# A 64-byte against a 192-byte start for x^T, and short matmuls ahead of twelve groups of products

## The chip, the cores and the metric

The kernel runs on one core of a Trainium2 chip. The metric is device time in microseconds (us) of one execution; the time before is the median of three runs, 2145.29 us (2144.81 to 2148.92).

## The reference

Two transformer blocks, one after the other, on 256 tokens of width 2048, all in fp32.

- The first block: RMS norm, a projection `h @ w_in` to 1024 + 2x128 + 3x1024 + 16 columns, a windowed attention with sinks (16 heads on 2 key heads) and a forgetting attention (16 heads), a norm of each, `concat @ w_out`, a residual; then norm, `h @ w_up` (2 x 5632 columns), a causal convolution of width 3 over the tokens, `gelu(gate) * val`, `@ w_down`, a residual.
- The second block: a modulation from `silu(c) @ w_ada`, norm, `h @ w_in_2` for the tokens and the key and value columns of it for 256 context tokens, rotary positions, windowed attention over tokens and context, a pooling path, `concat @ w_out_2`, a residual; then `square(relu(h @ w_mlp_up)) @ w_mlp_down` with 8192 inner columns, a residual and a last norm.

## The kernel before, in words

Every large product of fp32 matrices is made of three passes. Weights and activations are split into a high part (`hi`, rounded to the type fp32r) and a low part (`lo`, what is left), and each product adds hi x hi, hi x lo and lo x hi in a PSUM bank (`products`, L273 to L286 of the profile; all its matmuls have the line L285).

`run` works through a list of groups in order: v, kva, qa, qk0, qk1, wo_a0, wo_a1, wo_b0, wo_b1; up0, up1, up2, then twice-halved w_down groups (dn) that take two up groups each, between up groups: dn0, up3, up4, dn2, up5, up6, dn4, up7, up8, dn6, up9, up10, dn8; ckv, kv, q, u, wo2_p0, wo2_p1, wo2_a0, wo2_a1; mup0, mup1, mdn0, mup2, mdn1, and so on to mup7, mdn6, mdn7. A group's weights arrive in blocks of 1 MB by DMA on SP's queue into `raw` (four buffers); ScalarE rounds each half block into a `hi` tile (L156), VectorE subtracts for the `lo` tile (L168). Each of these has four buffers of 1088 elements of 4 bytes, used in rotation. PACE and `tick` place the side work (attention steps, the modulation's dot products, evacuations) between the halves of a block. The names in the trace are those of the groups without their number: the banks of up0 to up10 are b_up.

There are two kinds of product. In a feature-major one (op "A": kva, qa, qk, up, q, mup, half of ckv and kv) the stationary operand is a 128x128 slice of a weight tile and the moving one is x^T, 256 tokens wide; the trace shows it as `b_up<-a,hi` (moving, stationary). In a token-major one (op "B": v, wo, dn, u, mdn, the other half of ckv and kv) the moving operand is a weight slice of up to 512 columns and the stationary one is 128 tokens of x^T or of another activation; `b_dn<-hi,p`. Each matmul has its own weight load (engine PEld). A group of 1024 feature-major columns has 384 products: 16 slices of the contraction, four banks of two, three passes.

x^T is held as hi and lo tiles from `xt_tile` (L339 to L341), eight slices of 256 tokens to a tile. A tile has 2112 elements of 4 bytes, 8448 bytes, 33 x 256; x^T begins 16 elements, 64 bytes, into it. It is written by `make_ht` (L344): four transposes (L357) a bank, then ScalarE and VectorE. v, kva, qa, qk, up, ckv, kv, q, u and mup read it; wo, dn and mdn read other tiles, which begin at the tile's own start.

Other matmuls of TensorE stand between the products where side work has them: attention's steps in qk (L455, L456 scores on 64 rows; L499 transposes; L511, L514), the decay sums ahead of qa (L735 to L739), the transposes of `make_ht` in up0, mup0, ckv and kv. In up1 to up10 and in mup1 to mup7 there are none.

Of the kernel before, what the change touches and what calls it, by code (L numbers as in the profile page):

```python
# [9 lines left out]
F32R = mybir.dt.float32r  # L10
# [25 lines left out]


WARM = dict(up0=8, mup0=4)


class Group:
# [27 lines left out]
class Kernel:  # L69
# [51 lines left out]
    def run(self, groups):  # L121
        nc = self.nc
        blocks = [(g, b) for g in groups for b in range(g.nb)]
        raws, his, los = {}, [], []
        dma_p = [0]

        def dma_to(i):
            while dma_p[0] <= min(i, len(blocks) - 1):
                g, b = blocks[dma_p[0]]
                self.n += 1  # L130
                t = self.raw_p.tile([128, 2080], F32, tag="raw", name=f"raw{self.n}")
                t3 = t[:, :2 * g.kpc * g.width].rearrange("p (k f) -> p k f", f=g.width)
                if g.middle and b == 0:
                    g.load(t3[:, 0:1], 0)
                    g.between()
                    g.load(t3[:, 1:2], 1)
                else:
                    g.load(t3, b)
                raws[dma_p[0]] = t
                dma_p[0] += 1  # L140

        def part(j):
            i, u = divmod(j, 2)
            g = blocks[i][0]
            w = g.kpc * g.width
            return g.conv or (lambda d, r: [(d, r)]), raws[i][:, u * w:(u + 1) * w], w

        def hi_to(j):
            while len(his) <= min(j, 2 * len(blocks) - 1):
                dma_to(len(his) // 2 + 2)  # L150
                views, raw, w = part(len(his))
                self.n += 1
                hi = self.w_p.tile([128, 1088], F32R, tag="hi", name=f"hi{self.n}")[:, :w]
                with self.behind("hi"):
                    for h, r in views(hi, raw):
                        nc.scalar.copy(h, r)  # L156
                his.append(hi)

        def lo_to(j):
            while len(los) <= min(j, 2 * len(blocks) - 1):  # L160
                n = len(los)
                hi_to(n)
                views, raw, w = part(n)
                self.n += 1
                lo = self.w_p.tile([128, 1088], F32R, tag="lo", name=f"lo{self.n}")[:, :w]
                with self.behind("lo"):
                    for (l, r), (h, _) in zip(views(lo, raw), views(his[n], raw)):
                        self.dve.tensor_tensor(out=l, in0=r, in1=h.bitcast(F32), op=ALU.subtract)  # L168
                los.append(lo)

        banks = None
        for i, (g, b) in enumerate(blocks):
            last = b == g.nb - 1
            if last and g.tail:
                continue
            if not g.middle or b:
                lo_to(2 * i)
            if b == 0 and i and blocks[i - 1][0].tail and not g.prep:
                lo_to(2 * i + 3)
            fresh = b == 0 and i and blocks[i - 1][0].tail and g.prep  # L180
            if not fresh and (b or not g.middle):
                hi_to(2 * i + 3)
            if b == 0:
                self.pace = PACE[g.name] if g.name in PACE else PACE[g.name.rstrip('0123456789')]
                self.ticks = 0
                if not isinstance(self.pace, tuple):
                    self.wait = min(self.wait, self.pace)
                if g.before:
                    g.before()
                if g.side:  # L190
                    self.sides += g.side()
                banks = None
            if fresh:
                self.keep_warm(WARM[g.name], mm)
                g.prep(-2)
                self.held["hi"], self.held["lo"] = [self.ev[0]], [self.ev[1]]
                lo_to(2 * i + 1)
            if g.prep:
                g.prep(b)
            if fresh:  # L200
                hi_to(2 * i + 3)
            if banks is None:
                banks = [self.bank(g.name) for _ in g.banks]
            w2 = [(his[j], los[j]) if j < len(los) else None for j in (2 * i, 2 * i + 1)]

            def unit(bank, prog, u):
                for kk in range(g.kpc):
                    k = (2 * b + u) * g.kpc + kk
                    w = [t[:, kk * g.width:(kk + 1) * g.width] for t in w2[u]]
                    self.products(bank, prog, w, g.xs(k), k == 0, k == g.nk - 1)  # L210

            nb = len(banks)
            if g.tail and b == g.nb - 2:

                w2 = []
                for u in range(4):
                    lo_to(2 * i + u)
                    hi_to(2 * i + 3)
                    w2.append((his[2 * i + u], los[2 * i + u]))
                    for n in range(nb // 2):  # L220
                        unit(banks[n], g.banks[n], u)
                    self.tick(False)
                for n in range(nb):
                    if n >= nb // 2:
                        for u in range(4):
                            unit(banks[n], g.banks[n], u)
                    mm = self.mm
                    g.done(n, banks[n])
                continue
            if g.middle and b == 0:  # L230
                for tt in range(2):
                    if tt:
                        g.middle()
                    for u in range(2):
                        lo_to(2 * i + u)
                        w2[u] = his[2 * i + u], los[2 * i + u]
                        for n in range(nb // 2 * tt, nb // 2 * (tt + 1)):
                            unit(banks[n], g.banks[n], u)
                    hi_to(2 * i + 2 + tt)
                self.tick()  # L240
                lo_to(2 * i + 3)
                continue
            if not last:
                for u in range(2):
                    lo_to(2 * i + u)
                    hi_to(2 * i + u + 3)
                    w2[u] = his[2 * i + u], los[2 * i + u]
                    for bank, prog in zip(banks, g.banks):
                        unit(bank, prog, u)
                    self.tick()  # L250
                    lo_to(2 * i + u + 3)
                continue
            lo_to(2 * i + 1)
            w2 = [(his[j], los[j]) for j in (2 * i, 2 * i + 1)]
            for n, (bank, prog) in enumerate(zip(banks, g.banks)):
                unit(bank, prog, 0)
                unit(bank, prog, 1)
                if n == (nb - 1) // 2 and nb > 1:
                    self.tick()
                    lo_to(2 * i + 3)  # L260
                if g.done:
                    g.done(n, bank)
            self.tick()
            lo_to(2 * i + 3)
            if g.after:
                g.after(banks)
# [6 lines left out]
    def products(self, bank, prog, w, x, first, last):  # L273
        nc = self.nc
        (wh, wl), (xh, xl) = w, x
        for n, op in enumerate(prog):
            passes = ((wh, xh), (wh, xl), (wl, xh))
            for m, (ww, xx) in enumerate(passes):
                if op[0] == "A":
                    _, o, c = op  # L280
                    dst, lhsT, rhs = bank[:, o:o + 256], ww[:, c:c + 128], xx
                else:
                    _, o, w_, tt, c = op
                    dst, lhsT, rhs = bank[:, o:o + w_], xx[:, 128 * tt:128 * tt + 128], ww[:, c:c + w_]
                self.mm = self.pe.matmul(dst, lhsT, rhs, start=first and n == 0 and m == 0,  # L285
                                 stop=last and n == len(prog) - 1 and m == 2, skip_group_check=True)  # L286
# [51 lines left out]

    def xt_tile(self):  # L339

        return self.A8([128, 2112], F32R)[:, 16:16 + 2048].rearrange("p (k t) -> p k t", t=256)  # L341


    def make_ht(self, src, gain, shift=None):  # L344
# [1158 lines left out]
```

## Time and profile before

| what | value |
|---|---|
| median of three runs | 2145.29 us |
| profiled execution, its own time | 2145.99 us |
| span from first to last instruction | 2144.2 us |
| TensorE busy | 2119.4 us |
| VectorE busy | 1576.6 us |
| ScalarE busy | 1077.7 us |
| DMA | 491.39 MB, 229 GB/s in the mean |
| granted clock of TensorE, mean | 0.997 |

An engine's busy time is the union of its instructions' recorded durations. Those of matmuls overlap, as they are pipelined, and their ends are modelled; so the distance between the starts of two products, not their duration, says what a product costs.

### The profile page before, as it was taken

The numbers are of one execution on the slowest core, as the hardware profiler recorded it, in microseconds if no ns is written. First come the engines' busy times: TensorE is split into PE (matmuls) and PEld (weight loads), VectorE is DVE, ScalarE is ACT, GpSimd is POOL, SyncE is SP. The second block draws the span as 40 slices with busy tenths as digits, with TensorE's granted clock in tenths as the row PEclk, the third lists the DMA queues.
The fourth block names the chain that finished last, engine by engine and source line by source line (L and its number), as shares of the span: only waits on it lengthen the run. The fifth ranks groups of instructions, "written<-read, shape, count | busy, mean of one in ns | idle before, by whom it ended". The sixth has DMA issues, their size and how long they took to land.

```text
span 2144.2 us, 34901 instructions
## 1 busy us (share of the span) xinstructions
PE 2119.4 (99%) x14278; PEld 1928.9 (90%) x14278; DVE 1576.6 (74%) x2094; ACT 1077.7 (50%) x1557; POOL 39.3 (2%) x58
## 2 busy tenths in 40 slices
PE   8999999999999999999999999999999999999997
PEld 7998977999998999989989978889898998989986
DVE  6777688788679787797899797765656657555476
ACT  5446565555445543454566466454543434434343
POOL 0001000000000000000000000000000000000000
PEclk9999999999999999999999999999999999999999
DMA  8753576676767788787878754845767677555673
GB/s 308 267 181 136 157 226 227 217 255 225 258 232 248 256 284 305 267 318 278 278 278 283 274 168 158 216 157 181 251 205 273 212 248 246 189 197 179 196 233 101
DMA packets 120960, 491.39 MB, mean 229 GB/s; under 512 B 8736, under 2 KB 12640, under 8 KB 107360
## 3 DMA queue, kind: packets, MB, share of 16 engines
q1 hardware_dynamic: 120800, 489.16, 67.2%
q8 instruction: 112, 1.84, 0.3%
q14 instruction: 48, 0.39, 0.1%
HBM read 484.90 MB, written 2.13 MB: 227 GB/s over the span
## 4 chain that ended last, share of the span: by engine, by line
PE 96%; DVE 2%; ACT 1%; DMA 1%; issue 0%; POOL 0%; POOLq 0%; ACTq 0%; SPq 0%; DVEq 0%
PE b_up L285 23%; PE b_mup L285 17%; PE b_mdn L285 16%; PE b_dn L285 10%; PE b_qk L285 4%; PE b_wo_a L285 4%; PE b_v L285 2%; PE b_u L285 2%; PE b_qa L285 2%; PE b_q L285 2%; PE b_wo_p L285 2%; PE b_wo_b L285 2%; PE b_kv L285 1%; PE b_ckv L285 1%; PE b_aux L1202 1%; PE b_aux L1159 1%
## 5 line engine op out<-in xcount | busy, mean ns | idle before, releaser
L168 DVE TENSOR_TENSOR lo<-raw,hi 128x1024 fp32r<-128x1024 f32 (+2 forms) x716 | 850.4, 1199 | 448.6 <-ACT hi L156 447.1
L156 ACT CAST hi<-raw 128x1024 fp32r<-128x1024 f32 (+2 forms) x716 | 730.4, 1030 | 854.3 <-PE b_up L285 208.5
L285 PE MATMUL b_up<-a,hi 128*128 128x256 f32 x2816 | 499.8, 280 | 0.0
L285 PEld LDWEIGHTS b_up<-a,hi 128*128 128x128 f32 x2816 | 431.2, 188 | 0.5
L285 PE MATMUL b_up<-a,lo 128*128 128x256 f32 x1408 | 393.8, 280 | 0.0
L285 PE MATMUL b_mup<-a,hi 128*128 128x256 f32 x2048 | 363.0, 280 | 1.4 <-ACT a L374 1.4
L285 PE MATMUL b_mdn<-hi,p 128*128 128x512 f32 x1024 | 315.6, 389 | 0.0
L285 PEld LDWEIGHTS b_mup<-a,hi 128*128 128x128 f32 x2048 | 313.2, 187 | 2.1 <-ACT a L374 1.6
L285 PE MATMUL b_mup<-a,lo 128*128 128x256 f32 x1024 | 285.8, 279 | 0.0
L285 PEld LDWEIGHTS b_up<-a,lo 128*128 128x128 f32 x1408 | 265.3, 188 | 0.0
L587 DVE SCALAR_TENSOR_TENSOR raw<-raw,srow 128x2048 f32<-128x2048 f32 x96 | 219.6, 2287 | 25.0 <-DMA raw<-in_w_ada 24.7
L285 PEld LDWEIGHTS b_mdn<-hi,p 128*128 128x128 f32 x1024 | 191.7, 188 | 39.5
L285 PE MATMUL b_dn<-hi,p 128*128 128x512 f32 x704 | 217.2, 390 | 0.0
L285 PE MATMUL b_mdn<-lo,p 128*128 128x512 f32 x512 | 199.2, 389 | 0.0
L285 PEld LDWEIGHTS b_mup<-a,lo 128*128 128x128 f32 x1024 | 192.5, 188 | 0.0
L285 PEld LDWEIGHTS b_dn<-hi,p 128*128 128x128 f32 x704 | 131.6, 188 | 26.9
L285 PE MATMUL b_dn<-lo,p 128*128 128x512 f32 x352 | 137.1, 390 | 0.1
L285 PEld LDWEIGHTS b_mdn<-lo,p 128*128 128x128 f32 x512 | 96.1, 188 | 20.1
L285 PE MATMUL b_qk<-a,hi 128*128 128x256 f32 x512 | 93.4, 283 | 0.0
L285 PE MATMUL b_wo_a<-hi,a 128*128 128x512 f32 x256 | 80.3, 395 | 0.0
L285 PEld LDWEIGHTS b_qk<-a,hi 128*128 128x128 f32 x512 | 77.7, 188 | 2.6 <-issue 2.0
L285 PEld LDWEIGHTS b_dn<-lo,p 128*128 128x128 f32 x352 | 66.1, 188 | 14.4 <-DVE lo L168 0.6
(264 smaller groups left out, 2525.4 us busy)
## 6 DMA issues: line engine op xcount, KB each, us to landing
raw<-in_w_ada SPq DMA_DIRECT2D x96, 1024.0 KB, 5.6
raw<-in_w_up SPq DMA_DIRECT2D x88, 1024.0 KB, 5.0
raw<-in_w_mlp_up SPq DMA_DIRECT2D x64, 1024.0 KB, 5.0
raw<-in_w_mlp_down SPq DMA_DIRECT2D x64, 1024.0 KB, 5.7
raw<-in_w_in SPq DMA_DIRECT2D x50, 1024.0 KB, 5.9
raw<-in_w_down SPq DMA_DIRECT2D x44, 1024.0 KB, 6.2
raw<-in_w_out SPq DMA_DIRECT2D x32, 512.0 KB, 6.7
raw<-in_w_out SPq DMA_DIRECT2D x16, 1024.0 KB, 6.5
```

What stands on the lines that cost most here:

```text
L156: nc.scalar.copy(h, r)
L168: self.dve.tensor_tensor(out=l, in0=r, in1=h.bitcast(F32), op=ALU.subtract)
L285: self.mm = self.pe.matmul(dst, lhsT, rhs, start=first and n == 0 and m == 0, stop=last and n == len(prog) - 1 and m == 2, skip_group_chec ...
L587: self.dve.scalar_tensor_tensor(out=r, in0=r, scalar=1.0, in1=self.srow[0], op0=ALU.mult, op1=ALU.mult, accum_out=self.ada[:, f:f + 1])
L1159: self.pe.matmul(bk.rearrange("p (m c) -> p m c", m=2), qq, k.rearrange("p (m c) -> p m c", m=2)[:, :, o:o + 256], start=n == 0, stop=n == ...
L1202: self.pe.matmul(o[64 * s:64 * s + 64, 128 * qt:128 * qt + 128], v[:, c:c + 64], PT[x][:, 128 * kt:128 * kt + 128], start=kt == 0, stop=kt ...
```

## The change

x^T begins 48 elements, 192 bytes, into its tile instead of 16. And ahead of the first product of twelve groups stand one to four more matmuls (`LEAD`: rows, columns and moving columns of each and how many; 0 moving columns stands for a transpose of the identity). They write the first bank of the group, whose first product then starts it anew.

```diff
+LEAD = dict(qa=(128, 128, 128, 2), up2=(128, 128, 128, 1), up4=(128, 128, 128, 2), up6=(128, 128, 128, 4), up8=(128, 128, 0, 1), q=(128, 128, 64, 2),
+            mup2=(128, 128, 0, 2), mup3=(128, 128, 0, 4), mup4=(64, 128, 128, 1), mup5=(64, 128, 128, 2), mup6=(128, 128, 16, 1), mup7=(128, 128, 16, 4))
...
             if b == 0:
...
                 self.ticks = 0
+                self.lead = LEAD.get(g.name)
...
                     dst, lhsT, rhs = bank[:, o:o + 256], ww[:, c:c + 128], xx
+                    if self.lead:
+                        rows, cols, moving, times = self.lead
+                        self.lead = None
+                        for _ in range(times):
+                            if moving:
+                                self.pe.matmul(bank[0:cols, 0:moving], ww[0:rows, 0:cols], xx[0:rows, 0:moving], start=True, stop=True,
+                                               skip_group_check=True)
+                            else:
+                                self.pe.transpose(bank[:, 0:128], self.ident, self.ident)
...
-        return self.A8([128, 2112], F32R)[:, 16:16 + 2048].rearrange("p (k t) -> p k t", t=256)
+        return self.A8([128, 2112], F32R)[:, 48:48 + 2048].rearrange("p (k t) -> p k t", t=256)
```

## Rows read from the trace of the kernel before

**Rows 1.** The page: engines' busy time and share; chain that ended last, by engine.
```profile
PE 2119.4 (99%) x14278; PEld 1928.9 (90%) x14278; DVE 1576.6 (74%) x2094; ACT 1077.7 (50%) x1557; POOL 39.3 (2%) x58
...
PE 96%; DVE 2%; ACT 1%; DMA 1%; issue 0%; POOL 0%; POOLq 0%; ACTq 0%; SPq 0%; DVEq 0%
```

**Rows 2.** Two stretches: PE, PEld, DVE, ACT, POOL busy (count), PEclk, DMA share, GB/s.
```profile
960.20:1050.60 90.40, 90.40 (x769) 90.40 (x768) 65.72 (x71) 41.16 (x48) 0.00 (x0) 1.00 0.80 284
2000.80:2046.00 45.20, 45.20 (x385) 45.20 (x384) 20.12 (x17) 16.56 (x17) 0.00 (x0) 1.00 0.58 188
```

**Rows 3.** Timeline of TensorE in qk0: start us, duration us, what.
```profile
131.41 0.28 PE L285 MATMUL b_qk<-a,lo 128*128 128x256 f32 x1
...
133.88 0.28 PE L285 MATMUL b_qk<-a,lo 128*128 128x256 f32 x1
...
134.94 0.55 PE L499 MATMUL b_aux<-ident,p 128*128 128x128 f32 x3
...
135.56 0.28 PE L285 MATMUL b_qk<-a,lo 128*128 128x256 f32 x1
...
137.94 0.28 PE L285 MATMUL b_qk<-a,lo 128*128 128x256 f32 x1
```

**Rows 4.** By tile: count, duration ns min/median/max, first and last start us.
```profile
L285 PE MATMUL b_qk<-a,lo x7: 279/279/279, 148.8 to 150.9; 128*128 128x256 f32 x7
...
L285 PE MATMUL b_up<-a,lo x16: 280/280/282, 395.2 to 400.5; 128*128 128x256 f32 x16
...
L285 PE MATMUL b_qa<-a,lo x128: 278/280/280, 78.2 to 123.3; 128*128 128x256 f32 x128
```

**Rows 5.** Timeline of TensorE: decay sums ahead of qa; transposes in up0.
```profile
76.65 0.29 PE L735 MATMUL b_aux<-p,p 128*128 128x16 f32 x2
...
77.01 0.37 PE L737 MATMUL b_aux<-p,p 128*128 128x16 f32 x2
77.24 0.68 PE L738 MATMUL b_aux<-p,p 128*128 128x256 f32 x2
...
394.44 0.28 PE L285 MATMUL b_up<-a,lo 128*128 128x256 f32 x1
394.56 0.60 PE L357 MATMUL b_aux<-ident,a 128*128 128x128 f32 x4
...
395.24 0.28 PE L285 MATMUL b_up<-a,lo 128*128 128x256 f32 x1
```

**Rows 6.** Timeline of TensorE in qk0, score matmuls on 64 rows.
```profile
126.13 0.28 PE L285 MATMUL b_qk<-a,lo 128*128 128x256 f32 x1
126.34 0.48 PE L455 MATMUL b_aux<-p,p 64*128 64x128 f32 x2
126.66 0.59 PE L456 MATMUL b_aux<-p,p 64*128 64x256 f32 x2
...
127.53 0.28 PE L285 MATMUL b_qk<-a,lo 128*128 128x256 f32 x1
```

**Rows 7.** Timeline of TensorE in v and in u.
```profile
50.99 0.49 PE L285 MATMUL b_v<-hi,a 128*128 128x352 f32 x2
...
51.48 0.49 PE L285 MATMUL b_v<-hi,a 128*128 128x352 f32 x2
...
51.97 0.47 PE L285 MATMUL b_v<-hi,a 128*128 128x336 f32 x2
...
1215.65 0.39 PE L285 MATMUL b_u<-lo,a 128*128 128x512 f32 x1
...
1217.75 0.39 PE L285 MATMUL b_u<-lo,a 128*128 128x512 f32 x1
```

**Rows 8.** By tile: the products of mdn1 (columns as in Rows 4).
```profile
L285 PE MATMUL b_mdn<-lo,p x64: 389/389/395, 1602.6 to 1645.4; 128*128 128x512 f32 x64
```

**Rows 9.** Groups by line and shape: count, busy us, mean ns, idle before.
```profile
L285 PE MATMUL b_up<-a,lo 128*128 128x256 f32 x1408 | 393.8, 280 | 0.0
...
L285 PE MATMUL b_mup<-a,lo 128*128 128x256 f32 x1024 | 285.8, 279 | 0.0
```

## The prediction

> **What bounds the kernel now.** I read the page first: its busy line, the granted clock over the 40 slices and the chain that ended last. TensorE is busy for 99% of the span and is 96% of the chain [rows 1]. So the time is a sum of starts on TensorE: whatever shortens or lengthens the step from one product to the next is paid one for one, and nothing else is. Then I read busy time by stretch. A stretch of two feature-major groups, up9 and up10, b_up from 960.2 to 1050.6 us, holds 768 products in 90.4 us, 117.7 ns each, at a granted clock of 1.00 (the 2.4 GHz level); the last b_mup group, 384 products in 45.2 us, gives the same 117.7 ns. VectorE is busy for 65.7 of the 90.4 us, ScalarE for 41.2, the DMA engines for 80% [rows 2]. There are ten such stretches behind w_down and w_mlp_down groups, and all ten run at this pace. The reader is to see that here the engine is neither waiting nor slowed in its clock.
>
> Third, the timeline of TensorE inside b_qk, where attention matmuls cut the same kind of product into short stretches. It shows a second pace. From 131.41 to 133.88 us 21 steps take 2.47 us, 117.6 ns each; from 135.56 to 137.94, behind three transposes, 21 steps take 2.38 us, 113.3 ns each [rows 3]. Same shapes, same tiles, same x^T. So the step has two values, 4.4 ns apart, and the engine keeps the one it entered with: of the 27 stretches of b_qk behind other matmuls, nine run at the fast pace, from their second or third product to their end. What precedes the entry does not settle it alone: also behind three transposes, the stretch from 148.8 us stays slow; b_up behind four transposes is slow (nine such entries in b_up and b_mup, all slow), and so is all of b_qa behind narrow matmuls [rows 4]. In these rows the recorded duration of a product, 279 to 280 ns, marks the slow pace.
>
> **The change, part by part.**
>
> *Leads.* Twelve groups get 26 short matmuls in all (2+1+2+4+1+2 and 2+4+1+2+1+4). All stand on the chain. Each writes the bank that the first real product then clears, reads the weight tile and x^T that this product needs anyway, or the constant identity, and so adds no wait: what the first product waited for, the first lead waits for. It moves no DMA and no work of VectorE or ScalarE. Its price: four transposes of the identity kind put 0.80 us between two products that stand 0.353 us apart otherwise (394.44 to 395.24), so 0.112 us each; of 16-column matmuls the last two take 0.23 us (77.01 to 77.24), again about 0.112 each, and all six 0.59 us, 0.098 each [rows 5]. The column count hardly matters, each brings its own weight load. I take 0.112 for 23 of them: 2.6 us. The three leads on 64 rows are dearer: four 64-row matmuls of attention put 1.40 us between two products otherwise 0.353 apart, 0.262 us each [rows 6]; they stream more columns than the leads do, so this is a high value: 0.8 us. Sum 3.4 us; the ends are 26 x 0.098 = 2.5 us and 26 x 0.262 = 6.8 us.
>
> *What a lead can give back.* A group of 384 products that runs at 113.3 instead of 117.7 ns is 384 x 4.4 = 1.7 us shorter. Of the twelve groups only b_qa is cut by other matmuls of TensorE, once, so what is entered should last to the end of the group; the cover is there, since VectorE, ScalarE and the DMA engines have 20% or more left in rows 2 where 4% are needed. Whether a given lead lands in the fast pace the trace does not show: no short matmul of this operand type stands ahead of such a product. The nearest rows bound it: none of the nine entries behind four transposes, nine of 27 in b_qk [rows 3, 4]. The ends are 0 and 12 groups, 0 and 20.3 us. I take a quarter, three groups, 5.1 us, nearer to b_qk, because most leads are of the same operand type as the products, and no two groups have the same lead.
>
> Here a rule of the notes speaks against the change. The Trainium skill (TensorE: Matmul & The Clock Gate, section Step-by-step: what each phase is for) says that the moving operand and the weight load have independent read ports into SBUF, so that loading the next weights takes no read bandwidth from the running matmul. By it there is one pace, a lead is pure cost, and the sum is +3.4 us. The two paces of rows 3, at one granted clock, do not fit it, though they do not show that the ports are the reason.
>
> *The offset.* x^T moves by 128 bytes; no instruction is added or removed. Its price is in the pace of every product that reads it: as moving operand in the feature-major groups, as stationary one in b_v, b_u and half of b_ckv and b_kv. The best row is b_v: its weights are read in column groups that begin 0 and 1,408 bytes into the tile, and 1,408 is 128 past a multiple of 256. So the two groups already differ by just this shift between moving and stationary operand, and their triples take 0.49 us each (50.99 to 51.48, 51.48 to 51.97) [rows 7]. Hence I take zero. Both are slow: at the pace of b_mdn, 189 steps in 42.8 us or 226.5 ns for 512 columns [rows 8], three products of 352 columns would take 0.467. The bounds: b_u steps 233.3 ns (1215.65 to 1217.75, nine steps) against those 226.5, so 6.8 ns hang on each weight load there [rows 7, 8]; 192 products make 1.3 us, either way. For the feature-major products the ends are the fast pace for all and b_u's loss for all; they are rivals below.
>
> *Sum.* The profiled execution took 2145.99 us, its span 2144.2 and 1.8 around it, 0.7 above the median of the three runs, 2145.29. 2145.99 + 3.4 - 5.1 + 0 = 2144.3; set to the median, **2143.6 us**. With one to four groups landing, 2147.0 to 2141.9. About 0.2%, 4.3 us, is what a measurement of this kernel can tell from no change: below 2141.0 is faster, above 2149.6 slower.
>
> **The rivals.**
>
> *No lead lands: cost alone.* For it: nine entries of nine behind four transposes stayed slow, and all groups behind 512-column products do. Against: nine fast stretches in b_qk. 2145.3 + 3.4 = 2148.7, with the bounds 2147.8 to 2152.1. This is also what the rule of the skill cited above gives.
>
> *Most leads land*, five to twelve: if what counts is just that the first weight load falls beside a short matmul, all are alike. 2145.3 + 3.4 - 8.5 = 2140.2 down to 2145.3 + 3.4 - 20.3 = 2128.4.
>
> *The offset itself sets the fast pace everywhere.* b_up and b_mup have 3 x (1,408 + 1,024) = 7,296 products [rows 9], b_qa 384 [rows 4]: 7,680 x 4.4 = 33.8 us, so 2145.3 - 33.8 + 3.4 = 2114.9. For it: the pace depends on how two streams of reads meet, and the offset moves one of them. Against: b_v's two column groups.
>
> *The other side: the offset makes each product slower.* If relative position counts and its sense matters, a moving x^T 192 past the weights stands as b_u's weights stand now to a stationary x^T that is 64 past them; there each weight load costs 6.8 ns, where the feature-major step now pays 4.4. The difference, 2.4 ns on 7,680 products, is 18.4 us: 2145.3 + 18.4 + 3.4 = 2167.1. The place is every product of b_up and b_mup; it decides early: beyond the 3.4 us of the leads, 0.9 us more, or 0.12 ns a product, carries the time past 2149.6. Against it again b_v, and that b_u's products have 512 columns.
>
> That the leads do nothing because they are dropped can't be: they are plain matmuls in program order.
>
> **How the numbers follow.** Forecast (one to four land) 0.36; none lands 0.16; most land 0.21; offset fast 0.14; offset slow 0.13. Faster: 0.21 + 0.14 + 0.02 for four landing with cheap leads = 0.37. Slower: 0.13 + 0.04 of the cost-alone case at its dear end = 0.17. Same: the rest, 0.46. The range: its low end, 2126, holds "most land" with some room for b_u, and leaves out "offset fast" (0.14). Its high end, 2156, holds cost alone and half of "offset slow", whose 0 to 2.4 ns a product are all open; 0.06 stays out. The likeliest case alone has 2141.9 to 2147.0.
>
> **What would show it.** In the changed kernel's busy time by stretch, a group that landed takes 43.5 us for its 384 products, one that did not 45.2, and the recorded durations turn from 280 to 276. The groups without leads (b_up 1, 3, 5, 7, 9 and 10, b_mup 1) should still take 45.2 each: if they take 43.5, the offset did it; if they take more, the slow rival did. Starts of leads should stand 0.10 to 0.12 us apart. The forecast is wrong if the groups without leads change pace, if none or more than four of the twelve turn, or if a group loses its pace before its end.

## The result, and the profile after

The changed kernel takes 2135.1 us (median of four runs, 2133.43 to 2137.08); the kernel before, beside it, 2145.05 (2144.68 to 2148.92). The ratio is 0.995, its 95% interval 0.9933 to 0.9967: 10 us, 0.5% faster. The profiled execution took 2134.39 us, its span 2132.6, 11.6 below that of before.

The page of the changed kernel, engines' busy time and the chain that ended last, stands against [rows 1].

```profile
PE 2107.4 (99%) x14304; PEld 1917.0 (90%) x14304; DVE 1576.6 (74%) x2094; ACT 1077.9 (51%) x1557; POOL 40.2 (2%) x58
...
PE 95%; DVE 2%; ACT 1%; DMA 1%; issue 0%; POOL 0%; POOLq 0%; ACTq 0%; SPq 0%; DVEq 0%
```

TensorE has 26 instructions more and is busy 12 us less; VectorE and ScalarE have the same work. So the same products were taken at shorter steps. Busy time by stretch says where. Columns as in [rows 2]; in order the stretches are up3, up4, up9 with up10, q, mup1, mup2, mup3 and mup4 of the changed kernel.

```profile
554.90:600.10 45.20, 45.20 (x385) 45.18 (x384) 26.71 (x27) 19.25 (x23) 0.00 (x0) 1.00 0.67 239
600.30:643.90 43.60, 43.60 (x388) 43.60 (x386) 37.42 (x41) 22.02 (x27) 0.00 (x0) 1.00 0.66 228
955.97:1046.40 90.43, 90.43 (x769) 90.41 (x768) 66.12 (x71) 41.05 (x48) 0.00 (x0) 1.00 0.79 284
1166.40:1209.90 43.50, 43.50 (x385) 43.50 (x385) 31.86 (x43) 18.82 (x32) 0.00 (x0) 1.00 0.87 311
1461.20:1504.60 43.40, 43.40 (x385) 43.40 (x384) 24.32 (x25) 20.98 (x25) 0.00 (x0) 1.00 0.59 193
1548.30:1593.60 45.30, 45.30 (x387) 45.30 (x386) 21.97 (x20) 19.28 (x23) 0.00 (x0) 1.00 0.63 214
1637.50:1681.10 43.60, 43.60 (x387) 43.60 (x386) 22.30 (x21) 18.39 (x21) 0.00 (x0) 1.00 0.65 217
1725.00:1768.60 43.60, 43.60 (x385) 43.55 (x385) 22.29 (x21) 18.40 (x21) 0.00 (x0) 1.00 0.64 213
```

The granted clock is 1.00 in all of them, and the same 384 products take 45.2 or 43.5 us. Fast are up4, q, mup3, mup4 and, not shown, mup5, which have leads, and mup1, which has none. Of the other groups with leads mup2 is slow, and so are up2, up6, up8, mup6 and mup7; qa is fast for its first 48 products. The groups without leads up1, up3, up5, up7, up9 and up10 are slow as in [rows 2].

The recorded durations, by tile, mark the pace as in [rows 4]: up3, up4, and the last stretch of qk1.

```profile
L299 PE MATMUL b_up<-a,lo x125: 280/281/282, 555.5 to 599.3; 128*128 128x256 f32 x125
...
L299 PE MATMUL b_up<-a,lo x127: 275/276/277, 600.6 to 643.4; 128*128 128x256 f32 x127
...
L299 PE MATMUL b_qk<-a,lo x39: 275/276/279, 242.8 to 255.7; 128*128 128x256 f32 x39
```

In qk0 and qk1, which have no leads, 16 of the 27 stretches behind other matmuls end at the fast pace, where nine did before.

TensorE's timeline at the entries of up4, mup3 and mup4 (columns as in [rows 3]) shows what stands between the last product of the group before and the first of the new one.

```profile
600.03 0.28 PE L299 MATMUL b_up<-a,lo 128*128 128x256 f32 x1
600.14 0.33 PE L292 MATMUL b_up<-a,hi 128*128 128x128 f32 x2
600.31 0.45 PE L299 MATMUL b_up<-a,hi 128*128 128x256 f32 x2
...
1636.96 0.39 PE L299 MATMUL b_mdn<-lo,p 128*128 128x512 f32 x1
1637.19 0.60 PE L295 MATMUL b_mup<-ident 128*128 128x128 f32 x4
1637.54 0.48 PE L299 MATMUL b_mup<-a,hi 128*128 128x256 f32 x2
...
1724.48 0.39 PE L299 MATMUL b_mdn<-lo,p 128*128 128x512 f32 x1
1724.80 0.32 PE L292 MATMUL b_mup<-a,hi 64*128 64x128 f32 x1
1725.05 0.50 PE L299 MATMUL b_mup<-a,hi 128*128 128x256 f32 x2
```

Two leads of 128 columns push the first product of up4 back by 0.17 us, four transposes that of mup3 by 0.35. A single lead on 64 rows is dearer: it starts 0.32 us behind the last product, where mup3's first transpose starts at 0.23, and the first product comes 0.25 behind it. A further 0.06 to 0.11 us of each lies in the first steps after it: a fast group without leads takes 43.52 us, one behind leads 43.58 to 43.64.

By the distances between the first products of the groups, the 11.6 us are: up4, mup3, mup4 and mup5, 1.6 each, -6.4; q -2.0, mup1 -1.7, mup0 -1.2, v -1.7, qk0 and qk1 -0.9, u -0.5, up0 -0.4, kva and qa -0.4, together -8.8; and about +3.6, of which 0.6 stands in dn80, the first half of the last w_down groups, which differs by that much between runs, and the rest is what the leads cost elsewhere. So the larger part comes from groups that have no lead, and from q. The dn and mdn products keep their 226.7 ns.

### The profile page after: what moved, and what is told of

Its sections match the earlier page's. It is cut to its first block, busy times and chain, and to the rows that moved or that the text cites. A ratio compares the mean times of both kernels' runs of the same rounds, so it can differ in the third digit from the quotient of the medians.

```text
span 2132.6 us, 34950 instructions
## 1 busy us (share of the span) xinstructions
PE 2107.4 (99%) x14304; PEld 1917.0 (90%) x14304; DVE 1576.6 (74%) x2094; ACT 1077.9 (51%) x1557; POOL 40.2 (2%) x58
## 4 chain that ended last, share of the span: by engine, by line
PE 95%; DVE 2%; ACT 1%; DMA 1%; issue 0%; POOL 0%; POOLq 0%; ACTq 0%; SPq 0%; DVEq 0%
PE b_up L299 23%; PE b_mup L299 17%; PE b_mdn L299 16%; PE b_dn L299 9%; PE b_qk L299 4%; PE b_wo_a L299 4%; PE b_u L299 2%; PE b_qa L299 2%; PE b_wo_p L299 2%; PE b_q L299 2%; PE b_v L299 2%; PE b_wo_b L299 2%; PE b_ckv L299 1%; PE b_kv L299 1%; PE b_aux L1216 1%; PE b_aux L1173 1%
## 5 line engine op out<-in xcount | busy, mean ns | idle before, releaser
L299 PE MATMUL b_mup<-a,hi 128*128 128x256 f32 x2048 | 355.6, 279 | 1.3 <-ACT a L388 1.3
L598 DVE SCALAR_TENSOR_TENSOR p<-raw,srow 128x2048 bf16<-128x2048 f32 x32 | 73.2, 2289 | 9.3 <-DMA raw<-in_w_ada 9.1
```

Of the source, the lines that this page charges most:

```text
L598: self.dve.scalar_tensor_tensor(out=junk, in0=r, scalar=1.0, in1=self.srow[1], op0=ALU.mult, op1=ALU.mult, accum_out=self.adac[:, f:f + 1])
```

## The experiments

Each edit is against the changed kernel; in the cuts, lists of group names are written short. "Fast" is 113.3 ns a product (43.5 us for a group), "slow" 117.8 (45.2).

**The offset without leads.**

```diff
-LEAD = dict(qa=(128, 128, 128, 2), ...
+LEAD = {}
```

> x^T at 192 bytes, no lead. Theory (offset and leads act apart): v is 1.7 us shorter as in the changed kernel, kva, qa, qk, u, up0 and mup0 with mup1 together 5.0, all from the offset alone; up2 to up8, q and mup2 to mup7 stay at 117.8 ns; in all 2145.1 - 6.7 = 2138.4 us. Rival (the offset is what makes all fast groups fast): up4, q, mup3, mup4 and mup5 run at 113.3 without their leads as well, five times 1.65 us more, 2130.

Measured: 2137.97 us (2135.25 to 2139.68) against 2145.53; ratio 0.9967, interval 0.9955 to 0.998. Busy time by stretch, up2 and up3:

```profile
464.33:507.85 43.52, 43.52 (x386) 43.52 (x385) 39.33 (x50) 22.31 (x28) 0.00 (x0) 1.00 0.73 247
551.38:596.61 45.23, 45.23 (x385) 45.22 (x384) 27.18 (x29) 19.29 (x23) 0.00 (x0) 1.00 0.68 244
```

By tile, the products of q and of mup1:

```profile
L298 PE MATMUL b_q<-a,lo x128: 276/276/278, 1164.2 to 1207.4; 128*128 128x256 f32 x128
...
L298 PE MATMUL b_mup<-a,lo x127: 276/276/276, 1454.9 to 1497.8; 128*128 128x256 f32 x127
```

Without a lead anywhere, kva, the later part of up0, up1, up2, q and mup1 are fast, and qk is 0.9 us shorter. All groups that come straight behind dn or mdn, and those that follow these (up3 to up10, mup2 to mup7), stay at 45.23. So the offset alone is worth 7.6 us by the medians. The time is the theory's, its places are not: q and up2 were to stay slow. The offset acts where something other than a product of 512 columns stands ahead (transposes, attention, rotary matmuls), and the pace is then handed on: up1 and up2 take it from the end of up0.

What stands ahead can also turn a pace over. Four times in up0 and in mup0, behind their start, four transposes of `make_ht` stand between the products. In mup0 of the changed kernel, by tile, before the first of these entries, behind it, and behind the second:

```profile
L299 PE MATMUL b_mup<-a,lo x24: 275/276/277, 1418.0 to 1425.8; 128*128 128x256 f32 x24
...
L299 PE MATMUL b_mup<-a,lo x15: 280/281/282, 1426.9 to 1431.9; 128*128 128x256 f32 x15
...
L299 PE MATMUL b_mup<-a,lo x15: 276/276/278, 1433.0 to 1437.8; 128*128 128x256 f32 x15
```

So it goes fast, slow, fast, and then slow and fast again. In the nine profiles with x^T at 192 bytes, those of the kernels below among them, there are 72 such entries, and 69 turn the pace over; the other three are each the first of their group. In the three profiles at 64 bytes none of 24 does, and all are slow. How up0 and mup0 end thus hangs on the pace they begin with, which differs between runs. Below, with the 64-row leads behind dn and mdn alone, up0 ends slow, and no lead stands ahead of it there either.

**The leads without the offset.**

```diff
-        return self.A8([128, 2112], F32R)[:, 48:48 + 2048]...
+        return self.A8([128, 2112], F32R)[:, 16:16 + 2048]...
```

> x^T at 64 bytes as before, with the twelve leads. Theory (the kind of lead decides, whatever the offset): up4, q, mup3, mup4 and mup5 run at 113.3 ns, the other seven at 117.8; 5 x 1.65 gained, 3 us paid for the leads, 2145.1 - 5.2 = 2139.9 us. Rival (a lead lands only with the offset at 192): none of the twelve is fast, the leads cost 3 us, 2148.

Measured: 2144.5 us (2141.4 to 2146.22), ratio 0.9996, interval 0.9986 to 1.0005: no difference to be seen. Three groups are fast: up4, mup2 and mup6. Busy time of TensorE by stretch, mup2, mup3 and mup6:

```profile
1557.70:1601.30 43.60, 43.60 (x387) 1.00 0.65 221
1645.20:1690.50 45.30, 45.30 (x387) 1.00 0.61 206
1912.70:1956.30 43.60, 43.60 (x387) 1.00 0.59 191
```

At 192 bytes mup3, mup4 and mup5 land, at 64 bytes mup2 and mup6. The same lead at the same place lands at one offset and not at the other, so the two parts of the change don't act independently. Neither expectation held: the fast groups are others than the theory's, and they are not none. Three groups give back 5.1 us, the leads cost 3.6, and 1.5 us of gain is left to show, which this measurement can't tell from nothing.

**The changed kernel once more**, with nothing edited, to see whether an entry is chance.

> The changed kernel once more, nothing altered. In its first profile up4, q, mup1, mup3, mup4 and mup5 run at 113.3 ns a product, up2, up6, up8, mup2, mup6 and mup7 at 117.8. Theory (the pace is set at a group's entry by what stands there): the same groups at the same paces, 43.5 to 43.7 against 45.2 to 45.4 us each. Rival (chance at each entry): other groups are fast this time; two of these twelve or more change sides.

Measured: 2130.82 us in one run, span 2129.0. Eleven of the twelve groups with leads take the pace that they took before, to 0.01 us. The exception is up6, which is fast this time. The timeline of up5 (no lead of its own) and its tile's rows before and after the wait show how:

```profile
692.02 0.40 PE L299 MATMUL b_up<-a,hi 128*128 128x256 f32 x2
692.95 0.38 PE L299 MATMUL b_up<-a,lo 128*128 128x256 f32 x1 [0.53 <-DVE lo L172]
```

```profile
L299 PE MATMUL b_up<-a,lo x15: 281/281/281, 686.6 to 691.5; 128*128 128x256 f32 x15
...
L299 PE MATMUL b_up<-a,lo x109: 276/276/276, 693.8 to 730.5; 128*128 128x256 f32 x109
```

up5 enters slow, meets a wait of TensorE for VectorE's lo tile after some 50 products, goes on fast for the rest, and hands the pace to up6 through its four leads. So an entry is not drawn by lot; but a wait is an entry too, and waits differ from run to run.

**One kind of lead everywhere:** a single one on 64 rows, ahead of kva, qa, q, up1 to up10 and mup1 to mup7.

```diff
+LEAD = {n: (64, 128, 128, 1) for n in (kva qa up1 ... up10 q mup1 ... mup7)}
```

> x^T at 192 bytes, and one and the same lead, one matmul on 64 rows with 128 columns (that of mup4), ahead of each of 20 groups: kva, qa, up1 to up10, q, mup1 to mup7. Theory (the kind decides): all of up1 to up10, q and mup1 to mup7 run at 113.3 ns, 18 x 1.65 = 29.7 us gained, 20 x 0.3 paid for the leads, and 4 to 5 us of the offset in v, qk, u, up0 and mup0: about 2117 us. Rival (place decides as much as kind): some of these groups stay at 117.8, half of them would give about 2131.

Measured: 2128.82 us (2128.65 to 2129.56), ratio 0.9924, interval 0.991 to 0.9939. Busy time of TensorE by stretch, up3, up4 and mup2:

```profile
554.30:598.20 43.90, 43.90 (x386) 1.00 0.71 252
598.20:643.50 45.30, 45.30 (x385) 1.00 0.66 225
1547.70:1591.30 43.60, 43.60 (x385) 1.00 0.65 215
```

Behind dn and mdn this lead lands ten times out of ten, with the starts of the entries alike to 1 ns. Behind a feature-major group it turns the pace over, seven times of seven: up1, up4, up6, up8, up10 and mup1, each behind a fast end, are slow, and up2, behind the slow up1, is fast. So what stands ahead counts with the lead.

**The same lead behind dn and mdn alone** (up3, up5, up7, up9, mup2 to mup7).

```diff
+LEAD = {n: (64, 128, 128, 1) for n in (up3 up5 up7 up9 mup2 ... mup7)}
```

> x^T at 192 bytes; the lead of one matmul on 64 rows stands only ahead of the ten groups that follow token-major w_down or w_mlp_down products: up3, up5, up7, up9, mup2 to mup7. With it ahead of all groups those ten were fast, and up4, up6, up8, up10 and mup1, each behind a fast feature-major group, were slow. Theory (a group that follows another feature-major one keeps its pace unless other matmuls stand between, and the lead there threw it over): up4, up6, up8, up10 and mup1 run at 113.3 ns without a lead; ten times 1.25 net and four times 1.7 off the kernel with the offset alone, 2138.0 - 19.3 = 2118.7 us. Rival (these five are slow for their place): they stay at 117.8, 2125.5.

Measured: 2124.7 us (2123.61 to 2125.81), ratio 0.9912, interval 0.9896 to 0.9929. Busy time of TensorE by stretch, up3 and up4:

```profile
556.94:600.57 43.63, 43.63 (x386) 1.00 0.68 243
600.57:644.09 43.52, 43.52 (x387) 1.00 0.66 230
```

All ten groups with a lead are fast, and up4, up6, up8 and up10 are fast without any: one feature-major group hands its pace to the next. Each lead costs 0.45 us, 0.34 ahead of the first product and 0.11 in the first steps. up1, up2, mup1 and q, which hang on how up0, mup0 and the rotary matmuls end, are slow in this run (45.23 us, q 45.63). So the time is near the rival's, 2125.5, but of the five groups in question four run as the theory said, and mup1 alone is slow. q has no lead here and is slow, and in the next kernel too.

**Different kinds at those ten places** (one run).

```diff
+LEAD = dict(up3=(128, 128, 128, 1), up5=(128, 128, 128, 2), up7=(128, 128, 128, 4), up9=(128, 128, 64, 2), mup2=(128, 128, 64, 1),
+            mup3=(128, 64, 128, 1), mup4=(128, 128, 0, 1), mup5=(128, 128, 0, 3), mup6=(64, 128, 64, 1), mup7=(128, 128, 16, 2))
```

> x^T at 192 bytes; ahead of the same ten groups ten different leads: up3 one 128x128x128, up5 two, up7 four, up9 two with 64 columns, mup2 one with 64 columns, mup3 one on 128 rows and 64 output columns, mup4 one identity transpose, mup5 three, mup6 one on 64 rows with 64 columns, mup7 two with 16 columns. Theory (what decides is the delay between the last product and the first one's weight load, in steps of some ns): about half of the ten land at 113.3 ns, among them mup6, whose delay is that of the 64-row lead; each of up4, up6, up8, up10 has the pace of the group before it. Rival (only 64-row leads and four transposes land, because they interrupt the overlap of weight loads and products): mup6 alone lands.

Measured: 2126.05 us. Fast: up5 (two of 128 columns), up9 (two of 64), mup2 (one of 64), mup3 (one into 64 output columns), mup4 (one transpose). Slow: up3 (one of 128), up7 (four of 128), mup5 (three transposes), mup6 (64 rows, 64 columns), mup7 (two of 16). No order by count, columns or cost is left standing, and both expectations miss, as mup6 is slow. Delay orders them only if a few ns decide: the slow mup6 of the changed kernel and the fast mup2 here have their first and second products within 5 ns of each other behind the last mdn product (255 and 455 ns; 256 and 460). 5 ns is about what one step differs between the two paces, so delay is neither shown nor ruled out.

**Two other offsets, without leads** (`LEAD = {}`, one run each): x^T at a multiple of 256 bytes, and 128 past one.

```diff
-        return self.A8([128, 2112], F32R)[:, 48:48 + 2048]...
+        return self.A8([128, 2112], F32R)[:, 0:0 + 2048]...
...
-        return self.A8([128, 2112], F32R)[:, 48:48 + 2048]...
+        return self.A8([128, 2112], F32R)[:, 32:32 + 2048]...
```

> x^T at the tile's own start, no lead. Theory (the two paces come of how the reads of x^T and of the weights meet, and the offset sets which entry gives which): steps of 113.3 and 117.8 ns again, in other groups than at 64 or 192; behind w_down groups either all are fast or all slow. u and v, whose two operands then both begin at a multiple of 256 as in w_down's groups, come near w_down's pace, 226.7 ns for 512 columns. Rival (the offset by itself sets a pace): feature-major steps of a third value.

> x^T 128 bytes into its tile, no lead. Theory (as for x^T at the tile's start): steps of 113.3 and 117.8 ns, either all groups behind w_down fast or all slow, not the same entries as at 64 or 192. Rival (only the place within 128 bytes counts): every group as with x^T at the tile's start.

Measured: 2165.8 and 2162.53 us, against 2144.03. At offset 0 every feature-major group from qa on takes 120.0 ns a product (46.08 us) and none is ever fast. At 128 the pace is 118.7 in kva, qa, up0 to up2, q, mup0 and mup1 (45.56 us a group), 120.0 behind dn and mdn (46.08). So neither theory nor rival holds whole: at 0 there is one new value, at 128 two. By tile: the kernel at 0, part of up3 and up4.

```profile
L298 PE MATMUL b_up<-a,lo x213: 283/283/284, 563.3 to 639.7; 128*128 128x256 f32 x107
```

And the kernel at 128, up1 with up2, then up3 with up4:

```profile
L298 PE MATMUL b_up<-a,lo x239: 279/281/286, 425.0 to 509.7; 128*128 128x256 f32 x120
...
L298 PE MATMUL b_up<-a,lo x220: 281/285/286, 561.1 to 640.0; 128*128 128x256 f32 x110
```

So x^T's start has a price of its own that no lead makes: with no lead in either, 2145 us at 64, 2138 at 192, 2163 at 128 and 2166 at 0.

**One transpose at the ten places, and q's lead.**

```diff
+LEAD = dict(q=(128, 128, 64, 2), **{n: (128, 128, 0, 1) for n in (up3 up5 up7 up9 mup2 ... mup7)})
```

> x^T at 192 bytes; one identity transpose ahead of each of the ten groups behind w_down and w_mlp_down products (it landed ahead of mup4 in the kernel with ten kinds, at 0.03 us against 0.34 of the 64-row lead), and q's lead of two with 64 columns (q was fast with it twice). Theory (kind and the pace before it decide, not the group): all ten and with them up4, up6, up8, up10 run at 113.3 ns; 10 x 1.59 + 4 x 1.71 + 1.7 for q, 1.3 in kva and qk, 0.3 in u: 26 us off 2144.5, and up1, up2, mup0, mup1 as up0 and mup0 happen to end, 0 to 5 us more: 2114 to 2119. Rival (the group decides as well): some of the ten are slow, 1.6 us each and as much for the group behind it.

Measured: 2126.51 us (2124.62 to 2128.55), ratio 0.9917, interval 0.9902 to 0.9931. It lands at every second place: up3, up7, mup2, mup4, mup6 fast; up5, up9, mup3, mup5, mup7 slow. TensorE's timeline at up3 and at up5:

```profile
548.99 0.39 PE L298 MATMUL b_dn<-lo,p 128*128 128x512 f32 x1
549.22 0.27 PE L294 MATMUL b_up<-ident 128*128 128x128 f32 x1
549.25 0.48 PE L298 MATMUL b_up<-a,hi 128*128 128x256 f32 x2
549.57 0.28 PE L298 MATMUL b_up<-a,lo 128*128 128x256 f32 x1
...
679.69 0.39 PE L298 MATMUL b_dn<-lo,p 128*128 128x512 f32 x1
679.92 0.27 PE L294 MATMUL b_up<-ident 128*128 128x128 f32 x1
679.95 0.48 PE L298 MATMUL b_up<-a,hi 128*128 128x256 f32 x2
680.26 0.28 PE L298 MATMUL b_up<-a,lo 128*128 128x256 f32 x1
```

The two entries are alike to 0.01 us in the trace, and still up3's products are recorded with 276 ns and up5's with 281. To the ns they are not alike: the second product starts 461 or 462 ns behind the last dn or mdn product in the five fast groups, 457 or 458 in the five slow ones, which can be the cause of the pace or its first step. The place itself decides as well. The buffers of weights and x^T do not explain the alternation: every group and every pair of dn or mdn halves takes 16 half blocks, so with four buffers each entry begins with the same weight buffers, and x^T stands in the same tiles from up1 to up10. Nor does the pace before: up3 follows a fast up2 and is fast, up5 follows a fast up4 and is slow. What alternates stays open.

**Leads behind feature-major groups**, added to the ten transposes.

```diff
+LEAD = dict(up1=(128, 128, 128, 2), up4=(128, 128, 128, 2), up6=(128, 128, 64, 2), up8=(128, 64, 128, 1), up10=(128, 128, 128, 2),
+            mup1=(128, 128, 128, 2), q=(128, 128, 64, 2), **{the ten transposes})
```

> The kernel with the identity leads, and leads ahead of groups that follow a feature-major group as well: up4 and up10 two of 128x128x128 (slow to fast ahead of up4 in the changed kernel), up6 two with 64 columns, up8 one with 64 output columns, up1 and mup1 two of 128x128x128 behind a group whose pace is not known beforehand. Theory (what follows depends on the pace before the lead as well): of up4, up6, up8 and up10 some are thrown to 117.8 ns, 1.7 us each, and up4 and up10 agree, as they have one lead; about 2116 to 2124. Rival (a kind leads to one pace whatever was before): up4, up10, up1 and mup1 are all fast, 2113.

Measured: 2125.11 us (2124.72 to 2128.87), ratio 0.9909, interval 0.9893 to 0.9926. Busy time by stretch, up10 (two of 128 behind a slow up9) and up8 (one into 64 output columns behind a fast up7):

```profile
995.30:1038.90 43.60, 43.60 (x387) 43.60 (x386) 35.21 (x41) 22.74 (x29) 0.00 (x0) 1.00 0.78 273
861.00:906.20 45.20, 45.20 (x386) 45.20 (x385) 38.70 (x49) 22.66 (x29) 0.00 (x0) 1.00 0.79 279
```

Two of 128 columns keep a fast pace (up4) and make one of a slow one (up10, and up1 and mup1 behind an up0 and a mup0 that end slow). So the four groups of the rival are all fast, as it said; the time is longer than its 2113 because half of the transposes behind dn and mdn fail again and up8 is thrown to slow. up2, without a lead, takes the pace of up1 and loses it after 50 products, at a step of 0.94 us. Two of 128 columns is the kind to try everywhere.

**Two of 128 columns ahead of up1 to up10 and mup1 to mup7, and q's lead.**

```diff
+LEAD = dict(q=(128, 128, 64, 2), **{n: (128, 128, 128, 2) for n in (up1 ... up10 mup1 ... mup7)})
```

> x^T at 192 bytes; two matmuls of 128x128x128 ahead of each of 17 groups, up1 to up10 and mup1 to mup7, and q's lead of two with 64 columns. This kind has given the fast pace each time so far: ahead of up4 from a slow and from a fast group, ahead of up10 from a slow one, up1, mup1, and up5 behind w_down products. Theory (this kind leads to the fast pace from any entry): all 17 run at 113.3 ns, 17 x 1.7 less 17 x 0.2, q 1.6, kva and qk 1.3, u 0.3, up0 and mup0 1.5: about 2114 us. Rival (behind w_down products it alternates, as the identity did: up3, up7, mup2, mup4, mup6 fast with it and up5, up9, mup3, mup5, mup7 slow): five of the ten groups behind w_down or w_mlp_down stay slow, 1.7 us each, about 2122.

Measured: **2115.04 us** (2114.29 to 2116.06) against 2145.2; ratio 0.986, interval 0.9843 to 0.9876. It beats both kernels. TensorE is busy for 2088.3 us. Busy time by stretch, up2 and up3:

```profile
463.30:508.80 45.50, 45.38 (x387) 45.18 (x387) 40.44 (x51) 22.01 (x28) 0.00 (x0) 1.00 0.69 235
552.50:596.20 43.70, 43.70 (x388) 43.70 (x387) 26.94 (x30) 19.21 (x23) 0.00 (x0) 1.00 0.70 251
```

Sixteen of the 17 are fast to their end, behind dn, behind mdn and behind each other. up2 enters fast and loses the pace after 50 products, at a step of 0.40 us near 469 us; its tile's rows on both sides of it:

```profile
L298 PE MATMUL b_up<-a,lo x15: 276/276/280, 463.6 to 468.4; 128*128 128x256 f32 x15
...
L298 PE MATMUL b_up<-a,lo x110: 281/281/281, 469.8 to 508.3; 128*128 128x256 f32 x110
```

A pair costs 0.23 us, 0.17 ahead of the first product and 0.06 behind it, and a group gives back 1.7.

**The same leads at 64 bytes.**

```diff
+LEAD = dict(q=(128, 128, 64, 2), **{n: (128, 128, 128, 2) for n in (up1 ... up10 mup1 ... mup7)})
-        return self.A8([128, 2112], F32R)[:, 48:48 + 2048]...
+        return self.A8([128, 2112], F32R)[:, 16:16 + 2048]...
```

> The same 17 leads of two 128x128x128 and q's, x^T at 64 bytes as in the kernel before. With 192 bytes all 17 groups were fast, but for up2, which lost the pace inside: 2115.0 us. Theory (which kind lands hangs on the offset too: at 64 bytes up4 landed with this kind from a slow group, the identity pair and one with 16 columns landed elsewhere, 64-row ones not): the groups behind a feature-major one are fast, those behind w_down products may all be slow or all fast; kva, qa, qk, q as before; between 2119 and 2134 us. Rival (this kind leads to the fast pace at either offset): all 17 at 113.3 ns, 2118 with the kva, qk and q of before.

Measured: 2147.44 us (2146.55 to 2149.24), ratio 1.0012, interval 1.0003 to 1.0022. Only up2 is fast. Busy time by stretch, up2 and up3:

```profile
469.50:513.10 43.60, 43.60 (x387) 43.60 (x386) 37.79 (x50) 22.84 (x30) 0.00 (x0) 1.00 0.69 247
556.80:602.20 45.40, 45.40 (x388) 45.40 (x387) 27.15 (x30) 19.23 (x23) 0.00 (x0) 1.00 0.68 244
```

Both expectations miss: of 17 groups one is fast, where at 192 bytes 16 are. The same 36 leads are worth 30 us with x^T at 192 bytes, together with what the offset gives alone, and cost 2.5 at 64. This is where the two parts of the change are most clearly not independent; in the totals of the changed kernel they nearly add up (1.0 us for its leads alone, not clear of nothing, and 7.6 for the offset, against 10.0).

## Why the prediction was right and wrong

The time, 2135.1 us, is inside the range (2126 to 2156), and that is partly luck: the range was wide to hold the rivals as well. The likeliest time, 2143.6, was 8.5 us too high, the measured one lies below the likeliest case's 2141.9 to 2147.0, and "same" was given a larger chance (0.46) than "faster" (0.37). The mechanism was right in its first half, TensorE's steps and their two paces. It was wrong in the second, that the offset does nothing: the offset alone gave more than the leads that turned groups, after their cost. All three signs of a wrong forecast came: a group without a lead changed pace (mup1), more than four of the twelve groups run fast (up4, q, mup3, mup4 and mup5), and qa loses its pace before its end.

- **The bound.** TensorE's steps, paid one for one: held. The busy time of TensorE fell by 12.0 us, the span by 11.6.
- **Two paces at one clock, kept from the entry on.** Held, with two additions. A wait inside a group is an entry too: up5 of the repeated run gained the pace at one, up2 of the best kernel lost it. And the pace before an entry counts: at 192 bytes four transposes turned it over 69 times of 72. That "none of the nine entries behind four transposes" lands was true of 64 bytes only.
- **The leads' price.** Forecast 3.4 us. 23 leads at 0.112 hold (four of 16 columns push the products back by 0.444, two transposes by 0.229). The leads on 64 rows do not: a single one costs 0.45 us and a second behind it 0.12, so the three cost 1.0 instead of 0.8. In all 3.6.
- **How many land.** "One to four", three taken: up4, mup3, mup4 and mup5 turn, which don't in the kernel with the offset alone; qa, whose cut was taken to matter little, holds the pace for 48 products only, until two transposes. Each of the four gives 1.7 us as forecast, 1.6 when the leads' share inside the group is taken off. q turned too. Whether its lead did it is open: without a lead q is fast in the kernel with the offset alone and slow in two others at 192 bytes; with these leads it is fast in all five profiles at 192.
- **The offset at zero: this step failed.** "Hence I take zero" rested on b_v, whose two column groups differ by 128 bytes against x^T and take the same 0.49 us [rows 7]. The offset alone gave 7.6 us. The runs show in its place that the move from 64 to 192 leaves the slow pace at 117.8, and changes which entries turn to the fast one; moves from 64 to 0 and 128 do change the pace, to 120.0 at 0 and to 118.7 or 120.0 at 128. The row did not bear a zero, for it was read to 10 ns a triple, where 4.4 ns a product were at issue. To the ns the two triples of [rows 7] take 493 and 487. With x^T at 192 the medians of such triples, in the second half of v, are 480 and 482 (493 and 484 at 64). So b_v does change with the offset.
- **The sum** is mended by that term: 2145.05 + 3.6 - 6.8 - 7.6 = 2134.3, with 1.7 us for each of four groups; measured 2135.1. The fit is closer than the parts: up1 and up2, fast with the offset alone, are slow here, and mup0 and v are shorter here.
- **The rivals.** "No lead lands" is out. "Most leads land" would give the time (2128.4 to 2140.2), but not the places: besides q, whose lead may not be what turned it, four groups turn, and the rest of the gain stands in groups without leads. "The offset itself sets the fast pace everywhere" had the right cause and the wrong extent: groups behind 512-column products stay slow without a lead. "The offset makes each product slower" is what 0 and 128 do, at 2165.8 against 2144.0, +21.8 us, for 0; the price given for it, 18.4 us before the leads' cost, was near, for an offset that isn't the one of the change.

The rule set against the trace, two independent read ports for the moving operand and the weights (the Trainium skill, TensorE: Matmul & The Clock Gate, section Step-by-step: what each phase is for), would leave one pace whatever x^T's start. This case's traces have four, 113.3, 117.8, 118.7 and 120.0 ns, at a granted clock of 1.00 and with the same weights, so they do not agree with the one pace that was drawn from that rule. The measurement decides: where x^T stands matters to TensorE. That the ports are the place where the two reads meet is not shown.

What stays open is why x^T's start matters, and whether two reads meet at all. Entries that look alike to 0.01 us and have the same weight and x^T buffers differ, and the kind that lands differs between 64 and 192. The starts at 0 and 128 have one run each, but their 18 and 22 us are far beyond the spread of any kernel here. Not tried: other starts for the weights, different starts for the hi and lo x^T, starts that aren't multiples of 64 bytes. v varies at 192 bytes (52.75 to 54.77 us from kernel to kernel and run to run) and not at 64 (54.36 to 54.48), so the 1.7 us of the profiled run is not settled as the offset's.

## What to carry to other kernels

When TensorE is busy all the time at full clock, divide the distance of starts by the products, stretch by stretch: two values for one shape, as here, point to a pace that is kept, and what sets it can be moved. Try the start of the moving operand first, since it adds no instruction; try several, since two of the four here were 18 and 22 us slower. Only then try a pair of short matmuls at the entries that stay slow, with one kind tested at all of them; here the offset alone gave 0.3%, the leads that are best at 192 bytes nothing at 64, and both together 1.4%. Don't carry over the kind of lead: it held for one offset and one order of groups.

## What the runs showed of the hardware that was not expected

- The start of the moving operand in its tile, at 64-byte steps, changes the step of a 128x128x256 fp32r product with its own weight load: 120.0 ns at 0, 118.7 or 120.0 at 128, 117.8 (mostly) or 113.3 at 64, 117.8 or 113.3 at 192, all at a granted clock of 1.00.
- A pace lasts over hundreds of products and over the border of two groups of the same kind (up3 to up4 without a lead, 768 products), and turns at a wait of 0.53 us (up5 of the repeated run) as well as at other matmuls.
- With x^T at 192 bytes, four 128x128 transposes between such products turned the pace over in 69 of 72 entries; at 64 bytes in none of 24.
- Products of 512 columns between two such groups left the slow pace behind them in every case at 64 and 192 bytes, unless a lead followed.
- A lead on 64 rows between products on 128 rows costs 0.45 us, four times a lead on 128 rows; a second one right behind it costs 0.12.
